# First loads on two queues, two more block pairs per FFN, input forms without 1/rms, and head 0's softmax issued earlier

## The chip, the cores and the metric

The kernel runs on one core of a Trainium2 chip. Times are device microseconds of one execution: 2015.23 us is the median of three runs before the change (2014.92 to 2015.56). In the profile PE is the engine of the matmuls, PEld its weight loads, DVE, ACT and POOL the vector, scalar and GpSimd engines, SP the engine from whose queue nearly all loads are issued.

## The reference

The program is a trunk of two layers for 512 tokens of width 1024, all in float32:

```python
def rms_norm(x, g):
    return x * lax.rsqrt(jnp.mean(x * x, axis=-1, keepdims=True) + NORM_EPS) * g

def swiglu(x, w_gate, w_up, w_down):          # 1024 -> 2816 -> 1024
    return (jax.nn.silu(x @ w_gate) * (x @ w_up)) @ w_down

for layer in range(2):
    h = h + 0.5 * swiglu(rms_norm(h, ffn_norm[layer, 0]), ...)
    u = rms_norm(h, mix_norm[layer])
    h = h + (mla_gla_mixer(u, ...) if layer % 2 == 0 else nsa_mixer(u, ...))
    h = h + 0.5 * swiglu(rms_norm(h, ffn_norm[layer, 1]), ...)
return rms_norm(h, final_norm)
```

The NSA mixer has 16 heads of 64 in 4 groups. A head's output is the gated sum of three softmax branches: over 31 compressed keys, over selected key blocks, and over a window. For 512 tokens the selection and the window hold every causal key, so the last two branches are plain causal softmaxes over their own keys.

## The kernel before

Activations lie transposed, features on the 128 partitions and the 512 tokens along the row; x is eight tiles `x0` to `x7`. To keep float32 accuracy every operand is split in a high and a low part, and `mm3` (lines 145 to 147) makes each product of three matmuls: high by high, high by low, low by high. `split` (lines 150, 151) makes the parts: ACT casts the high one, DVE subtracts it to get the low one. Each weight tile (`raw`, 512 KB, three buffers) is loaded by SP's queue and split so.

There are four FFNs, FFN0 to FFN3; the MLA and GLA mixer stands between the first two, the NSA mixer between the last two. An FFN has 22 column blocks of 128, each a gate and an up product, called a pair here. Pairs come in two kinds.

A whole pair (`whole`, j < `NP` = 6) has two products of 8 by 3 matmuls with 512 columns, from x times the gain alone (`xs`, made by `ffn_input`); 1/rms (`rb`) is not needed for these, and comes in when DVE evicts them (line 386, `gt` and `ut`). The first eviction thus waits for `rb`, and since the tag `gu` has four PSUM banks, two for a pair, the third whole pair waits for the first eviction.

A block pair (`gate_up` and `gate_up_steps`, the other 16) is a two-by-two block product in Winograd's form: seven products of 12 matmuls with 256 columns in place of eight. It needs sums of weights (`sa`, `sb`, lines 130 to 133, and their splits `shi`, `slo`) and seven forms of the input (`ffn_forms`). The forms are made from x times gain times `rb`, 16 operations on DVE at line 282, three subtractions, and seven splits. At a pair's end ACT applies Silu to each half of `gt` (lines 334, 349), DVE multiplies (`done`, line 363), and `hid[j]` is split for the down product.

Down products (`unit`, `ps_d`) of a group of four or five finished pairs are put between the pairs of the next group, and the last group's run behind the last pair. FFN3 ends in `ffn_end`, which works on halves of the tokens with the last four `hid`.

The order of instructions on each engine is fixed when the program is built, by a list scheduler that goes by a model of ready times and priorities. `tc.high_priority(AHEAD)` moves a few evictions ahead, `issue_after` holds an instruction back in this order. `bufs=n` says how many buffers a tag shares: a load into `raw` waits until the tile three loads earlier has been read.

In the NSA mixer `nsa_keys_queries` makes the projections row by row; after row `CMP_AFTER` it issues `cmp_probs`, the compressed branch's probabilities of the first group. `nsa_attend` then runs the heads; `probs(h)` holds a head's 14 score matmuls, its softmax blocks, and POOL's weighing by the gates (line 584).

At the start SP issues all loads: x0, the gains, the first weight in four parts, x1 to x7, then masks and tables, and only then the second weight.

Of the kernel before, what the change touches and what calls it, by code (L numbers as in the profile page):

```python
# [29 lines left out]
NP = 6  # L30
# [9 lines left out]
class Core:  # L40


    def __init__(self, ctx, tc, a):
        self.ctx, self.tc, self.nc, self.a = ctx, tc, tc.nc, a
        nc = self.nc
        ep = lambda name, bufs, **k: ctx.enter_context(tc.tile_pool(name=name, bufs=bufs, **k))
        self.cp = ep("const", 1)
        self.xp = ep("resid", 1)
        self.sp = ep("scr", 1)
        self.wp = ep("wts", 1, side="right")  # L50
        cp = self.cp
# [4 lines left out]
        self.inv_dm = self.const_col(1.0 / DM, "inv_dm")  # L56
        table = cp.tile([P, 1], F32, name="table")
        nc.scalar.activation(table, self.ones[:, :1], AF.Identity, scale=self.inv_dm)
        self.gains = cp.tile([P, 7, KC], F32, name="gains")
        self.x = []  # L60
        for k in range(KC):
            self.x.append(self.xp.tile([P, T], F32, name=f"x{k}"))
        self.open_sums()
# [5 lines left out]
    def load_x(self, k0, k1):  # L69
        for k in range(k0, k1):  # L70
            self.nc.sync.dma_start(out=self.x[k], in_=self.a["xT"][:, k])
# [164 lines left out]
    def ffn(self, f, gi, meanwhile=None, out=None, act_last=False):  # L236

        if f:
            self.open_sums()
        with self.fws, ExitStack() as st:  # L240
            if act_last:
                hp = st.enter_context(self.pool("hid"))
            self.open_act(st, 14)
            self.open_psum(st, gu=4, d=3, st=1)
            if not act_last:
                hp = st.enter_context(self.pool("hid"))
            fp = st.enter_context(self.pool("fin")) if out is not None else None
            self.ffn_body(f, gi, hp, meanwhile, fp, out)
# [22 lines left out]
    def ffn_forms(self, gi, hp, parts):  # L271

        V = self.nc.vector
        b11, b12, b21, b22, t = (hp.tile([P, 4, H], F32, name="xf", tag="hid", bufs=HID) for _ in range(5))
        for kh, bs in enumerate(((b11, b12), (b21, b22))):
            for th, b in enumerate(bs):
                for kk in range(4):
                    k = 4 * kh + kk  # L280
                    ts = slice(th * H, th * H + H)
                    V.scalar_tensor_tensor(
                        out=b[:, kk], in0=self.x[k][:, ts], scalar=self.gains[:, gi, k : k + 1], in1=self.rb[:, ts], op0=ALU.mult, op1=ALU.mult,
                    )
            yield

        def add(b):
            parts.append((self.form("bh"), self.form("bl")))
            self.split(b, *parts[-1])

        V.tensor_sub(t, b22, b12)
        add(b11)
        yield
        add(b21)
        add(t)
        yield
        V.scalar_tensor_tensor(out=t, in0=t, scalar=-1.0, in1=b11, op0=ALU.mult, op1=ALU.subtract)
        V.scalar_tensor_tensor(out=b21, in0=t, scalar=-1.0, in1=b21, op0=ALU.mult, op1=ALU.subtract)
        V.tensor_sub(b12, b11, b12)
        yield  # L300
        for b in (t, b21, b12, b22):
            add(b)

    def product(self, ps, w, x, start=False):

        for kk in range(4):
            m = slice(kk * P, (kk + 1) * P)
            self.mm3(ps, w[0][:, m], w[1][:, m], x[0][:, kk], x[1][:, kk], start and kk == 0, kk == 3, skip_group_check=True)

    def gate_up_steps(self, hp, w, x, done):  # L310
# [37 lines left out]
        with tc.high_priority(AHEAD):  # L348
            S.activation(gt[:, H:], z, AF.Silu)
        done(gt, ut)  # L350

    def ffn_body(self, f, gi, hp, meanwhile, fp, out):
# [5 lines left out]
        acc = self.sumsq(self.x, fast=True) if self.first else None  # L358
# [3 lines left out]
        def done(j, gt, ut):  # L362
            V.tensor_mul(ut, gt, ut)
# [3 lines left out]
        def whole(j):  # L367
# [14 lines left out]
            if self.rb is None:  # L382
                self.rb = self.norm_stats(acc)[1]
# [19 lines left out]
        making = self.ffn_forms(gi, hp, forms)  # L403
# [638 lines left out]
class Mix1(Mix0):  # L1042
    def ffn_mix1(self):

        a = self.a
        with ExitStack() as left, ExitStack() as right:
            with self.pool("rope1", side="right") as tp:
# [3 lines left out]
                with ExitStack() as pj:  # L1051
# [3 lines left out]
                    with self.pool("cmp") as cq:  # L1055
                        rb = self.nsa_cmp(mp, cq, xh, xl)
                        self.nsa_gates(mp, cq, xh, xl, rb)
                    self.open_act(left, 16, "kq")
                    ks, qs = self.nsa_keys_queries(mp, xh, xl)
            at = right.enter_context(self.pool("nsa_at", side="right"))  # L1060
            self.open_psum(right, s=3, pt=3, av=1, pj=1)
            oh, ol = self.nsa_attend(mp, at, ks, qs)
# [164 lines left out]
    def nsa_keys_queries(self, mp, xh, xl):  # L1227
# [31 lines left out]
        for row, scale, store, args in steps:  # L1259
# [7 lines left out]
        return ks, qs  # L1267
# [41 lines left out]
    def nsa_attend(self, mp, at, ks, qs):  # L1309
# [4 lines left out]

        def probs(h):

            g = h // 4
            sums = at.tile([P, 2, 4], F32, name="sums", tag="sums", bufs=2)
            kh, kl = ks[g]
            out = [at.tile([P, 1280], F32, name="pr", tag="pr", bufs=4) for _ in range(2)]  # L1320

            def block(br, qb, ps):
                n = (qb + 1) * P
                self.softmax_block(ps, n, out[br][:, OFF[qb] : OFF[qb] + n], sums[:, br, qb : qb + 1], mp, "f")

# [172 lines left out]
```

## Time and profile before

| | |
|---|---|
| median of 3 runs | 2015.23 us |
| the profiled execution's own time | 2016.61 us |
| its span, first to last instruction | 2014.6 us |
| PE busy | 1969.8 us (98%) |
| DVE busy | 1496.0 us (74%) |
| ACT busy | 1020.9 us (51%) |
| POOL busy | 212.8 us (11%) |
| mean granted TensorE clock | 0.990 |

The profile shows one execution; a row of the timeline gives the start from the span's beginning, the length, the engine, the source line, what was written from what, and in brackets how long the engine had stood idle and what released it. Matmuls overlap, so the time of one is read from start to start, not from its length.

### The profile page before, as it was taken

The page shows a single profiled execution, that of the slowest core. Times are in us where ns is not written, and L with a number is a line of the kernel's source. Part 1 is how long each engine was busy: PE and PEld are TensorE (multiplying, and loading weights), DVE is VectorE, ACT ScalarE, POOL GpSimd, SP SyncE. Part 2 cuts the span into 40 slices and gives each one's busy share as a digit, 9 for nine tenths or more (in the row PEclk, how much of TensorE's full clock was granted, in tenths as well). Part 3 has the DMA queues.
Part 4 walks back from the last instruction along what each step waited for, and adds up shares of the span by engine and source line. Part 5 has one row for each costly group of instructions (what it writes and reads, how often), then busy time and mean ns, then how long its engine had stood idle before and what let it go on. Part 6 is the DMA issues. An engine that isn't in the chain of part 4 may idle for free.

```text
span 2014.6 us, 31364 instructions
## 1 busy us (share of the span) xinstructions
PE 1969.8 (98%) x11934; PEld 1737.3 (86%) x11934; DVE 1496.0 (74%) x2571; ACT 1020.9 (51%) x1850; POOL 212.8 (11%) x258
## 2 busy tenths in 40 slices
PE   8999999999999999999999999999899999999997
PEld 6899999898778899998789999888687878999997
DVE  7877775688888677775877777677899868777764
ACT  6444443665674444444544444445588754444443
POOL 0000000201340000001000000111266510000002
PEclk9999999999999999999999999999899999999999
DMA  5233322321313232323323233354400133233332
GB/s 173 89 98 102 101 96 79 109 74 44 88 66 113 89 101 90 117 91 89 121 89 96 94 106 103 90 146 135 116 2 1 33 112 97 86 102 96 102 96 67
DMA packets 71910, 186.40 MB, mean 93 GB/s; under 512 B 9936, under 2 KB 13648, under 8 KB 71760
## 3 DMA queue, kind: packets, MB, share of 16 engines
q1 hardware_dynamic: 71760, 184.41, 29.5%
q8 instruction: 93, 1.52, 0.3%
q14 instruction: 57, 0.47, 0.1%
HBM read 172.84 MB, written 2.10 MB: 87 GB/s over the span
## 4 chain that ended last, share of the span: by engine, by line
PE 89%; DVE 5%; ACT 2%; issue 1%; DMA 1%; SPq 1%; POOL 0%; DVEq 0%; ACTq 0%; POOLq 0%
PE ps_d L145 8%; PE ps_d L146 8%; PE ps_d L147 8%; PE ps_a L145 6%; PE ps_a L147 6%; PE ps_a L146 6%; PE ps_b L145 5%; PE ps_b L147 5%; PE ps_b L146 5%; PE ps_gu L146 5%; PE ps_gu L145 5%; PE ps_gu L147 4%; PE ps_p L145 3%; PE ps_p L146 2%; PE ps_p L147 2%; PE ps_pt L593 2%
## 5 line engine op out<-in xcount | busy, mean ns | idle before, releaser
L150 ACT CAST whi<-raw 128x512 fp32r<-128x512 f32 (+4 forms) x319 | 257.7, 811 | 333.5 <-PE ps_d L146 126.6
L151 DVE TENSOR_TENSOR wlo<-raw,whi 128x512 fp32r<-128x512 f32 (+4 forms) x319 | 308.2, 968 | 84.6 <-ACT whi L150 83.6
L145 PE MATMUL ps_d<-hid,whi 128*128 128x512 f32 x672 | 265.1, 398 | 0.0
L146 PE MATMUL ps_d<-hid,whi 128*128 128x512 f32 x672 | 264.2, 394 | 0.0
L147 PE MATMUL ps_d<-hid,wlo 128*128 128x512 f32 x672 | 263.9, 394 | 0.0
L145 PE MATMUL ps_a<-bh,shi 128*128 128x256 f32 x768 | 217.0, 282 | 0.0
L146 PE MATMUL ps_a<-bl,shi 128*128 128x256 f32 x768 | 216.4, 282 | 0.0
L147 PE MATMUL ps_a<-bh,slo 128*128 128x256 f32 x768 | 216.2, 281 | 0.0
L215 POOL TENSOR_TENSOR ssq<-ssq,sq 128x512 f32<-128x512 f32 x30 | 46.3, 1545 | 1093.9 <-ACT sq L214 1093.9
L147 PEld LDWEIGHTS ps_d<-hid,wlo 128*128 128x128 f32 x672 | 126.1, 188 | 30.4 <-DVE wlo L151 0.7
L145 PEld LDWEIGHTS ps_d<-hid,whi 128*128 128x128 f32 x672 | 126.1, 188 | 26.4 <-ACT whi L150 1.0
L146 PEld LDWEIGHTS ps_d<-hid,whi 128*128 128x128 f32 x672 | 126.1, 188 | 24.4
L146 PEld LDWEIGHTS ps_a<-bl,shi 128*128 128x128 f32 x768 | 144.8, 189 | 1.2
L145 PEld LDWEIGHTS ps_a<-bh,shi 128*128 128x128 f32 x768 | 144.1, 188 | 1.3
L147 PEld LDWEIGHTS ps_a<-bh,slo 128*128 128x128 f32 x768 | 145.0, 189 | 0.0
L130 DVE TENSOR_TENSOR sa<-raw 128x512 f32<-128x512 f32 x64 | 44.2, 690 | 130.7 <-DMA raw<-wgu 130.6
L398 DVE SCALAR_TENSOR_TENSOR x<-ps_d,x 128x512 f32<-128x512 f32 x152 | 104.2, 687 | 44.1 <-PE ps_d L147 43.8
L584 POOL TENSOR_TENSOR pr<-pr,sums 128x128 f32<-128x128 f32 (+3 forms) x160 | 114.4, 747 | 106.7 <-DVE sums L1342 42.6
L150 ACT CAST uhi<-raw 128x512 fp32r<-128x512 f32 x64 | 39.7, 621 | 163.5 <-PE ps_b L146 102.9
L150 ACT CAST shi<-sa 128x1024 fp32r<-128x1024 f32 x64 | 67.2, 1050 | 81.5 <-PE ps_a L146 73.0
L151 DVE TENSOR_TENSOR slo<-sa,shi 128x1024 fp32r<-128x1024 f32 x64 | 78.3, 1224 | 33.5 <-ACT shi L150 33.4
L565 ACT ACTIVATE pr<-sm_s,sm_m 128x512 f32<-128x512 f32 (+3 forms) x160 | 90.2, 565 | 17.4 <-DVE sm_m L561 13.4
(448 smaller groups left out, 5583.6 us busy)
## 6 DMA issues: line engine op xcount, KB each, us to landing
raw<-wgu SPq DMA_DIRECT2D x175, 512.0 KB, 3.8
raw<-wd SPq DMA_DIRECT2D x96, 256.0 KB, 2.7
raw<-wd SPq DMA_DIRECT2D x64, 320.0 KB, 3.0
raw<-wo SPq DMA_DIRECT2D x32, 256.0 KB, 2.8
raw<-w1t SPq DMA_DIRECT2D x16, 512.0 KB, 3.7
raw<-w0v SPq DMA_DIRECT2D x8, 512.0 KB, 3.6
raw<-w0t SPq DMA_DIRECT2D x6, 512.0 KB, 3.9
rt_s<-rt_f SPq DMA_DIRECT2D x48, 64.0 KB, 2.0
```

The costliest lines, as they stand in the source:

```text
L130: V.tensor_add(av[:, :w], g[:, :w], u[:, :w])
L145: mm(ps, lh, rh, start=start, stop=False, **k)
L146: mm(ps, lh, rl, start=False, stop=False, **k)
L147: mm(ps, ll, rh, start=False, stop=stop, **k)
L150: self.nc.scalar.copy(hi, src)
L151: self.nc.vector.tensor_sub(lo, src, f32v(hi))
L215: (nc.vector if last or fast else nc.gpsimd).tensor_add(acc, acc, sq)
L398: V.scalar_tensor_tensor(out=self.x[c], in0=ps, scalar=0.5, in1=self.x[c], op0=ALU.mult, op1=ALU.add)
L565: nc.scalar.activation(p, s[:, :n], AF.Exp, bias=mn, scale=-1.0, accum_out=sums)
L584: self.nc.gpsimd.tensor_mul(o, o, w[:, qb : qb + 1].to_broadcast([P, n]))
L593: self.nc.tensor.transpose(ps[:, off : off + P], prs[br][:, o : o + P], self.ident)
```

## The change

The first loads use two queues: ACT issues x0, x1 and x2 with x3, SP the gains, the first weight in two parts, x4 with x5 and x6 with x7. Eleven small matmuls of ones by ones are issued ahead of FFN0's first product. `NP` is 4, so each FFN has 4 whole and 18 block pairs. The forms of the input are made without `rb`: three of the seven are views of `xs`, four are made from x times gain by one operation or more, and `rb` is multiplied in at the end of a block pair: DVE multiplies `gt` by it, POOL multiplies `ut`, ACT applies Silu over the full width, and POOL makes the product of both. `nsa_probs` of head 0 is issued inside `nsa_keys_queries`, with the PSUM tag `ch`; the later `cmp_probs` are held back behind the preceding head's score matmuls. The kernel is built with a DMA scratch size of 1024.

```diff
-NP = 6
+NP = 4
+WARM = 11
...
+        load(nc.scalar, 0, 1)
+        nc.sync.dma_start(out=self.gains, in_=a["gains"])
+        load(nc.scalar, 1, 2)
+        self.first = self.wload(a["wgu"][0, 0, 0], 1024, parts=2)
+        load(nc.scalar, 2, 4)
+        load(nc.sync, 4, 6)
+        load(nc.sync, 6, 8)
...
-        self.load_x(0, 1)
-        nc.sync.dma_start(out=self.gains, in_=a["gains"])
-        self.first = self.wload(a["wgu"][0, 0, 0], 1024, parts=4)
-        self.load_x(1, KC)
...
-            self.open_act(st, 14)
+            self.open_act(st, 17 if out is not None else 16)
...
+        for kk in range(4):
+            S.activation(b12[:, kk], block(kk, 1), AF.Copy, scale=gain(kk))
+        parts.append(view(0, 0))
+        parts.append(view(1, 0))
+        combine(t3, 1, 1, b12, ALU.subtract)
+        form(t3, False)
         yield
+        combine(t2, 0, 0, t3, ALU.add)
+        form(t2, True)
         yield
+        combine(t2, 1, 0, t2, ALU.subtract)
+        form(t2, True)
         yield
+        combine(b12, 0, 0, b12, ALU.subtract)
+        form(b12, False)
+        parts.append(view(1, 1))
...
             V.tensor_add(gt[:, :H], vv, sa)
-            S.activation(gt[:, :H], gt[:, :H], AF.Silu)
...
         with tc.high_priority(AHEAD):
-            S.activation(gt[:, H:], z, AF.Silu)
+            S.copy(gt[:, H:], z)
+        V.tensor_mul(gt, gt, self.rb)
+        nc.gpsimd.tensor_mul(ut, ut, self.rb)
+        S.activation(gt, gt, AF.Silu)
         done(gt, ut)
...
         def done(j, gt, ut):
-            V.tensor_mul(ut, gt, ut)
+            (V if j < NP else nc.gpsimd).tensor_mul(ut, gt, ut)
...
+        if f == 0:
+            ps = self.ps("warm", "st")
+            for _ in range(WARM):
+                nc.tensor.matmul(ps[:, :P], self.ones, self.ones, start=True, stop=True)
...
             if row == CMP_AFTER:
                 self.pc0 = self.cmp_probs(mp, qs, 0, "ch")
+                first = self.nsa_probs(mp, self.ap, ks, qs, 0, "ch")
...
-                    pc[(h + 1) // 4] = self.cmp_probs(mp, qs, (h + 1) // 4, "pj")
-                nxt = probs(h + 1)
+                    with self.tc.issue_after(end.ins):
+                        pc[(h + 1) // 4] = self.cmp_probs(mp, qs, (h + 1) // 4, "pj")
+                nxt = self.nsa_probs(mp, at if (h + 1) % 3 else self.ap, ks, qs, h + 1, "s")
```

Three places show how the instructions move. The first is DVE in FFN1, around the first eviction (`gt` from `ps_gu`; line 386 before, 397 after). Before:

```order
L202 TENSOR_SCALAR rs_q<-rs_q 128x4
L203 TENSOR_TENSOR rc<-rc,rs_q 128x4
L182 TENSOR_SCALAR dg<-ident,rc 128x128 x4
L151 TENSOR_TENSOR wlo<-raw,whi 128x1024
L386 TENSOR_TENSOR gt<-ps_gu,rb 128x512
L386 TENSOR_TENSOR ut<-ps_gu,rb 128x512
```

After:

```order
L203 TENSOR_TENSOR rc<-rc,rs_q 128x4
L182 TENSOR_SCALAR dg<-ident,rc 128x128 x4
L151 TENSOR_TENSOR wlo<-raw,whi 128x1024
L130 TENSOR_TENSOR sa<-raw 128x512
L131 TENSOR_TENSOR sa<-raw 128x512
L397 TENSOR_TENSOR gt<-ps_gu,rb 128x512
L397 TENSOR_TENSOR ut<-ps_gu,rb 128x512
```

The `wlo` is that of the fourth pair's gate weight in both; the two sums of pair 5's weights now stand between it and the eviction. FFN2 has the same rows.

The second is ACT at the end of FFN3's last pair (`gt` from `ps_a`, then the cast of its `hid`; `keep` are the last down weights, `facc` the final norm's first square). Before:

```order
L150 CAST keep<-raw 128x512
L334 ACTIVATE gt<-gt 128x256
L339 COPY sx<-ps_a 128x256
L150 CAST keep<-raw 128x512 x3
L349 ACTIVATE gt<-ps_a 128x256
L150 CAST hid<-ut 128x512
```

After:

```order
L150 CAST keep<-raw 128x512 x2
L358 COPY gt<-ps_a 128x256
L361 ACTIVATE gt<-gt 128x512
L150 CAST hid<-ut 128x512
L473 ACTIVATE facc<-x 128x256
```

Between the last read of `ps_a` and the cast of `hid` there is now a full-width Silu on ACT, with DVE's product by `rb` ahead of it and POOL's product behind it.

The third is PE where the NSA projections end: `ps_s` are a head's scores, `ps_sc` and `ps_sct` belong to a group's compressed probabilities, `ps_pc` to their transposes, `ps_av` to the values. Before:

```order
L1304 MATMUL ps_pc<-ident,sc_s 128x128 x4
L1328 MATMUL ps_s<-kh,q 128x256
L1329 MATMUL ps_s<-kl,q 128x256
L1337 MATMUL ps_s<-kh,q 128x256
...
L1353 MATMUL ps_av<-pcl,vcz 128x512
L1279 MATMUL ps_sc<-q,kcwh 128x512
...
L1284 MATMUL ps_sct<-ident,sc_t 128x128 x4
L1337 MATMUL ps_s<-kh,q 128x512
```

After:

```order
L1321 MATMUL ps_pc<-ident,sc_s 128x128 x4
L1339 MATMUL ps_s<-kh,q 128x256
L1340 MATMUL ps_s<-kl,q 128x256
L1348 MATMUL ps_s<-kh,q 128x256
...
L1349 MATMUL ps_s<-kl,q 128x384
L1369 MATMUL ps_av<-pch,vcz 128x512
L1370 MATMUL ps_av<-pcl,vcz 128x512
L608 MATMUL ps_pt<-ident,pr 128x128 x2
```

The second group's `ps_sc` and `ps_sct` no longer stand among head 0's scores; the scores themselves still begin behind `ps_pc`.

## Rows read from the trace of the kernel before

**Rows 1.** Page, parts 1 and 4: busy time by engine, chain by engine.

```profile
PE 1969.8 (98%) x11934; PEld 1737.3 (86%) x11934; DVE 1496.0 (74%) x2571; ACT 1020.9 (51%) x1850; POOL 212.8 (11%) x258
...
PE 89%; DVE 5%; ACT 2%; issue 1%; DMA 1%; SPq 1%; POOL 0%; DVEq 0%; ACTq 0%; POOLq 0%
```

**Rows 2.** Stretches: core's length, then busy us of each engine, clock, DMA share, GB/s.

```profile
200.00:345.00 145.00, 145.00 (x984) 134.11 (x983) 99.00 (x145) 61.11 (x104) 0.00 (x0) 1.00 0.31 95
```

**Rows 3.** Timeline of PE: start, length, matmul, [idle before]; a whole and a block pair.

```profile
624.05 0.40 PE L145 MATMUL ps_gu<-xh,whi 128*128 128x512 f32 x1
...
629.65 0.40 PE L145 MATMUL ps_gu<-xh,shi 128*128 128x512 f32 x1
...
252.54 0.28 PE L145 MATMUL ps_a<-bh,shi 128*128 128x256 f32 x1
...
253.98 0.28 PE L145 MATMUL ps_a<-bh,whi 128*128 128x256 f32 x1
```

**Rows 4.** Timeline of PE and of SP's queue in FFN0's first 40 us.

```profile
9.17 0.79 PE L145 MATMUL ps_gu<-xh,whi 128*128 128x512 f32 x1 [2.12 <-ACT xh L265]
...
15.15 0.43 PE L145 MATMUL ps_gu<-xh,whi 128*128 128x512 f32 x1
...
10.00 0.33 SPq L91 DMA_DIRECT2D raw<-wgu  x1
...
38.12 0.50 PE L145 MATMUL ps_gu<-xh,whi 128*128 128x512 f32 x1 [1.64 <-DVE gt L386]
```

**Rows 5.** Stretches, as rows 2: hand-over from projections to attention, and attention.

```profile
1440.00:1470.00 30.00, 22.45 (x83) 15.99 (x82) 25.41 (x68) 18.30 (x47) 11.96 (x14) 0.66 0.26 64
...
1500.00:1575.00 75.00, 70.50 (x438) 59.07 (x437) 72.02 (x229) 66.43 (x184) 45.40 (x64) 1.00 0.01 1
```

**Rows 6.** Lines: sx's copy (200 to 345 us); POOL's sums, ns min/median/max.

```profile
L339 ACT COPY sx<-ps_a 128x256 f32<-128x256 f32 x9 | 3.3, 370 | 0.9 <-PE ps_a L147 0.8
...
L215 POOL TENSOR_TENSOR ssq<-ssq,sq x30: 1288/1476/2350, 356.0 to 1642.1; 128x512 f32<-128x512 f32 x30
```

**Rows 7.** Line 226's durations; timeline of POOL and DVE near 365 us.

```profile
L226 DVE SCALAR_TENSOR_TENSOR xl<-x,gains,xh x16: 739/742/1786, 356.4 to 1312.8; 128x512 fp32r<-128x512 f32 x16
...
364.71 2.35 POOL L215 TENSOR_TENSOR ssq<-ssq,sq 128x512 f32<-128x512 f32 x1 [1.76 <-ACT sq L214]
...
364.69 1.21 DVE L151 TENSOR_TENSOR wlo<-raw,whi 128x1024 fp32r<-128x1024 f32 x1
...
365.82 1.78 DVE L226 SCALAR_TENSOR_TENSOR xl<-x,gains,xh 128x512 fp32r<-128x512 f32 x1
```

**Rows 8.** Timeline of PE, DVE and ACT at the end of FFN3's pairs.

```profile
1977.43 0.28 PE L147 MATMUL ps_a<-bh,slo 128*128 128x256 f32 x1
...
1978.16 0.69 DVE L363 TENSOR_TENSOR ut<-gt,ut 128x512 f32<-128x512 f32 x1 [2.83 <-ACT gt L349]
...
1978.89 0.62 ACT L150 CAST hid<-ut 128x512 fp32r<-128x512 f32 x1 [0.76 <-DVE ut L363]
...
1979.56 0.62 PE L145 MATMUL ps_d<-hid,keep 128*128 128x256 f32 x3 [0.30 <-ACT hid L150]
```

**Rows 9.** Timeline of PE at the end of FFN0's pairs.

```profile
348.24 0.28 PE L147 MATMUL ps_a<-bh,slo 128*128 128x256 f32 x1
...
351.39 0.86 PE L145 MATMUL ps_d<-hid,whi 128*128 128x512 f32 x3
```

**Rows 10.** Timeline of DVE in FFN1; page, part 6: loads of gate and up weights.

```profile
618.70 1.23 DVE L151 TENSOR_TENSOR wlo<-raw,whi 128x1024 fp32r<-128x1024 f32 x1 [1.60 <-ACT whi L150]
...
622.31 0.69 DVE L386 TENSOR_TENSOR gt<-ps_gu,rb 128x512 f32<-128x512 f32 x1 [2.39 <-ACT rb L167]
...
raw<-wgu SPq DMA_DIRECT2D x175, 512.0 KB, 3.8
```

**Rows 11.** Stretches, as rows 2, behind two waits of PE.

```profile
38.00:48.00 10.00, 9.88 (x42) 8.00 (x43) 10.00 (x23) 5.62 (x8) 0.00 (x0) 1.00 0.16 52
...
376.90:380.40 3.50, 3.50 (x19) 3.50 (x19) 2.48 (x11) 0.95 (x2) 0.00 (x0) 0.52 0.46 147
```

More of the change, by code (lines that the diff above doesn't have):

```diff
@@ L269, in ffn_input, with ffn_forms, view, combine @@
         return xs, end
[L271 to L292, printed above, removed]
+    def ffn_forms(self, gi, hp, xs, parts):
+        V, S = self.nc.vector, self.nc.scalar
+        b12, t3, t2 = (hp.tile([P, 4, H], F32, name="xf", tag="hid", bufs=HID) for _ in range(3))
+        gain = lambda k: self.gains[:, gi, k : k + 1]
+        block = lambda k, th: self.x[k][:, th * H : th * H + H]
+        def view(kh, th):
+            return [tuple(t[:, th * H : th * H + H] for t in xs[4 * kh + kk]) for kk in range(4)]
+        def combine(out, kh, th, t, op):
+            for kk in range(4):
+                k = 4 * kh + kk
+                V.scalar_tensor_tensor(out=out[:, kk], in0=block(k, th), scalar=gain(k), in1=t[:, kk], op0=ALU.mult, op1=op)
+        def form(t, negated):
+            h, l = self.form("th"), self.form("tl")
+            if negated:
+                S.activation(h, t, AF.Copy, scale=-1.0)
+                V.scalar_tensor_tensor(out=l, in0=t, scalar=-1.0, in1=f32v(h), op0=ALU.mult, op1=ALU.subtract)
+            else:
+                self.split(t, h, l)
+            parts.append([(h[:, kk], l[:, kk]) for kk in range(4)])
+        for kk in range(4):
+            S.activation(b12[:, kk], block(kk, 1), AF.Copy, scale=gain(kk))
[3 more added lines that the diff above has]
+        form(t3, False)
@@ L1307, in cmp_probs, with nsa_probs, block, nsa_attend @@
         return ph, pl
-    def nsa_attend(self, mp, at, ks, qs):
+    def nsa_probs(self, mp, pool, ks, qs, h, tag):
+        V, mm = self.nc.vector, self.nc.tensor.matmul
+        sums = mp.tile([P, 2, 4], F32, name="sums", tag="sums", bufs=3)
+        kh, kl = ks[h // 4]
+        out = [pool.tile([P, 1280], F32, name="pr", tag="pr", bufs=2 if pool is self.ap else 4) for _ in range(2)]
+        def block(br, qb, ps):
+            n = (qb + 1) * P
+            self.softmax_block(ps, n, out[br][:, OFF[qb] : OFF[qb] + n], sums[:, br, qb : qb + 1], self.ap, "sm")
+        ps = self.ps("ps_s", tag)
+        o = ps[:, : 2 * P].rearrange("p (b n) -> p b n", b=2)
+        mm(o, qs[h][:, :P], kh[:, :, :P], start=True, stop=False)
+        mm(o, qs[h][:, :P], kl[:, :, :P], start=False, stop=True)
+        for br in range(2):
+            block(br, 0, ps[:, br * P : (br + 1) * P])
+        for br in range(2):
+            for qb in range(1, 4):
+                n = (qb + 1) * P
+                ps = self.ps("ps_s", tag)
+                qt = qs[h][:, qb * P : n]
+                mm(ps[:, :n], qt, kh[:, br, :n], start=True, stop=False)
+                end = mm(ps[:, :n], qt, kl[:, br, :n], start=False, stop=True)
+                block(br, qb, ps)
+            w = sums[:, br]
+            V.scalar_tensor_tensor(out=w, in0=w, scalar=TINY, in1=self.inv_gates[:, h, br], op0=ALU.max, op1=ALU.mult)
+            V.reciprocal(w, w)
+            self.weigh(out[br], w)
+        return out, end
+    def nsa_attend(self, mp, at, ks, qs, nxt):
         nc, a = self.nc, self.a
```

66 lines of the change are left out of this document (14 added, 52 removed).

## The prediction

> **What bounds the kernel now.** I read the busy shares first, then the chain that ended last, then every idle gap of PE in the timeline, then the stretches around the edits. PE is busy 1969.8 of 2014.6 us and is 89% of the chain [rows 1]; DVE has 74%, ACT 51%, POOL 11%. So only two things can save time: fewer PE cycles, or shorter waits of PE, which stands still 44.8 us in all, with the stretches at its lower clock around them. Work on DVE, ACT or POOL counts only where PE waits for it. Inside the steady part of the FFNs PE never waits: in 200 to 345 us it is busy 145.00 of 145.00 while DVE has 99.00 and ACT 61.11 [rows 2]. The gaps lie at the start, at the first evictions of FFN0, in the small stages of the mixers and above all where the NSA projections hand over to attention.
>
> **The change part by part.** Times are against the profiled execution, span 2014.6 us; the median of the runs, 2015.23, is 0.63 above that span, and I add that at the end.
>
> *Two more block pairs in each FFN.* A whole pair is 48 matmuls of 512 columns; 24 of them take 629.65 − 624.05 = 5.60 us, so a pair takes 11.20. A block pair is 7 products of 12 matmuls of 256 columns; 12 take 253.98 − 252.54 = 1.44, so a pair takes 10.08 [rows 3]. Saved: 1.12 a pair, times 2 pairs, times 4 FFNs: **−8.96**. This is PE time proper, and the order of the products within a pair is unchanged. DVE pays more for a block pair's weights: three splits of 1024 and five operations of 512, 3 × 1.23 + 5 × 0.69 = 7.1 [rows 8, 10], where a whole pair has two splits, 2.5; twice an FFN, 9.2. The new forms give most of that back: seven splits and three full-size sums become four splits, six times 1.23 = 7.4 less, and they no longer wait for 1/rms. PE never waited for them, so this is 0 while DVE has its 31% idle; without that cover the rest, 1.8 an FFN, would be the price.
>
> *The start.* Before, PE has three matmuls from 5.34, waits 2.12 for x1 and runs on from 9.17; the second weight is asked for at 10.00, behind x, cmask and the rope table on SP; matmuls stand 0.43 apart up to 15.15 and 0.23 after, the two clock levels [rows 4]. Now x comes on two queues in larger pieces, u0 is asked for around 5, and 11 small matmuls run ahead. The first 24 products, of which nine are left at 15.15 before and end near 17.3, end near 16.0 by my walk, and the wait for slo behind them goes. The end of whole(1), its rb chain and the first eviction, for which PE waits 1.64 at 38.12 [rows 4], follow as a block; behind them two sums for pair 5 now stand ahead of that eviction, worth about 0.25. I take **−1.3**. Bounds: 0 if both queues share the same bandwidth and x1 comes as late as before; −3.5 if PE runs from 5.6 on or is at the upper clock from 9 on (13 matmuls by 0.2 = 2.6, and the rest from the waits).
>
> *NSA.* The diff speaks of head 0 among the projections; the order says otherwise: its 14 score matmuls still stand behind the last projection and the four ps_pc transposes. What leaves the hand-over is the second group's compressed probabilities: 8 score matmuls, 8 transposes, about 2.7 us of PE and 5 us of DVE, which go into attention. The 30 us from 1440 to 1470 have DVE busy 25.41, so 4.6 idle, and PE busy 22.45 at a mean clock of 0.66; attention behind it has DVE 72.02 of 75 and PE 70.50 [rows 5]. Work moved from a stretch where DVE is nearly full to one where both are nearly full can win at most the idle time, 4.6, plus some clock; it loses where the moved part splits a head's softmax: +2. Head 0's first sums come about 5.5 to 6.5 earlier by DVE's queue, 5 are paid back. I take **−2**.
>
> *The end of a block pair.* Now ACT copies (sx's copy: 0.370), DVE multiplies gt by rb, ACT does Silu over the full width, and POOL does ut·rb and gt·ut. POOL's 128x512 sums took 1.288 to 2.350, median 1.476 [rows 6]. In 72 pairs that is 2 × 1.48 × 72 = 213 us on an idle engine. Two costs follow.
>
> First, the two engines hold each other up. An xl, made from x and xh in SBUF, has a median of 742 ns but 1786 at most, and that one, from 365.82, lies beside a POOL sum of 2.35 from 364.71, itself 1.06 over the shortest. The wlo begun at 364.69 has its usual 1.21 [rows 6, 7]. Read in order: POOL stood behind wlo, then xl behind POOL. So each of POOL's two operations can cost DVE from 0 to 1.29, and I take 0.75 of that, the share of DVE's operations with both inputs in SBUF (an estimate from its list): 1.9 per pair. Nine pairs end in the 145 us [rows 2, 6], 16.1 each, so DVE goes from 68% to about 80%: **0**, covered by PE.
>
> Second, hid of the last pair comes later. In FFN3 the last ps_a matmul begins at 1977.43, gt·ut on DVE at 1978.16 (0.69), and ps_d's first use of that hid at 1979.56, after a wait of 0.30 [rows 8]. Now the chain is copy 0.37, gt·rb 0.69, Silu 0.62 (as hid's cast of that width [rows 8]), POOL 1.29, hid 0.62 with their hand-overs: about 1981.5. **+2.0**, all on the path since what lies ahead of it in PE's order is used up. In FFN0 the last ps_a begins at 348.24 and the first use of its hid stands at 351.39, so 3.15 of other products cover it [rows 9]; the chain needs 0.37 + 0.69 + 0.62 + 1.29 + 0.62 and four hand-overs of 0.1: 4.0. **+0.9** in each of three FFNs, **+2.7**. Bounds: 0.5 to 2.0 each, the upper one where POOL's product stands behind a DVE split as in rows 7, 1.06 more.
>
> [...]
>
> *The first evictions of FFN1 and FFN2.* Pair 5's two sums (lines 130, 131) now stand ahead of the first gt eviction on DVE, and they need the twelfth raw tile, u5. Its buffer comes free only when wlo of g3 has been made: 618.70 + 1.23 = 619.93 in the trace of before. A 512 KB load takes 3.8 from issue to landing [rows 10], so u5 lands at 623.7, the sums end at 625.0, the eviction at 625.7. Before, the eviction is at 622.31 [rows 10] and whole(2) starts at 624.05 with no wait [rows 3]. Queued behind: that eviction and through it PE. **+1.6** in FFN1 and, by the same order, FFN2: **+3.2**. Bounds 0 (load in 2.2) and +5 (load crowded). In FFN3 the first eviction stands ahead of those sums, so nothing.
>
> *The DMA scratch size* changes no instruction: 0.
>
> Sum: −8.96 − 1.3 − 2.0 + 2.0 + 2.7 + 3.2 = −4.36, a span of 2010.2 and a median of **2010.9**.
>
> **Rivals.** *A, the new waits are covered:* u5 lands in time and the three FFN tails keep 0. Then −8.96 − 1.3 − 2.0 + 2.0 = −10.3, and with the start's better end −12.5: 2003 to 2005. For it: 3.8 is a median over loads in busier stretches too, and PE had no wait at either place. Against: both chains are sums of serial steps, each from a row.
>
> *B, the clock falls behind the new waits (slower).* [...] Behind the wait of 1.64 at 38.12 [rows 4] it stays at 1.00 [rows 11]; PE had wide matmuls before that one. The change adds six waits of 0.9 to 2 us (four tails, two evictions). [...] By its surroundings a tail or eviction is like 38.12, so I give this little. [...]
>
> *C, NSA gives nothing or loses* (the change does not do there what it says): the second group's probabilities cost attention 5 us of DVE, the hand-over gains 5: C between 0 and +2 in place of −2: 2013 to 2015, not to be told from no change.
>
> **How the numbers follow.** A measurement tells 0.2%, 4 us. Chances: forecast 0.46 (own range 2007.5 to 2014, by the bounds of start, tails and evictions), A 0.18, B 0.15, C 0.21. Faster by over 0.2% means under 2011.2: A whole and 0.7 of the forecast, whose median lies there, 0.18 + 0.32 = 0.50. Slower means over 2019.3: the upper half of B, 0.08, and 0.04 of C for a DVE-bound attention: 0.12. Same: 0.38. The range leaves out half of A's faster end and B's upper part: 2003.5 to 2018.
>
> **What would show it.** In the trace of the changed kernel: a pair in FFN2 from 11.20 to 10.08; PE waits for hid of about 2.3 in FFN3 and about 0.9 in the others; waits of about 1.6 for gt in FFN1 and FFN2 with the L130 sums after a raw load just ahead on DVE; DVE's two-SBUF operations longer beside POOL but PE full in the pairs; the ps_s waits at the hand-over smaller and those inside attention larger; first full-rate matmul before 15. I am wrong if PE waits inside the pairs (DVE bound), if the tails show no wait, or if the granted clock has new dips.

## The result

The changed kernel takes 2029.45 us (median of five runs, 2025.9 to 2030.76), the kernel before 2015.56 in the same session: a ratio of 1.0063, 95% interval 1.0051 to 1.0074. It is slower by 13.9 us where 4.4 faster was forecast. The profiled execution is one of the quicker ones, 2026.95 with a span of 2025.2, so the traces have 10.6 us to explain. The rest lies in the spread of the runs. The medians here are of undisturbed runs; one run of the experiment with the old start, 3461.16 us at a granted clock of 0.768, is left out.

Parts 1 and 4 of the page of the changed kernel, the engines' busy time and the chain that ended last (of before in [rows 1]):

```profile
PE 1966.1 (97%) x12244; PEld 1747.2 (86%) x12244; DVE 1557.1 (77%) x2597; ACT 1047.2 (52%) x1900; POOL 425.1 (21%) x402
...
PE 84%; DVE 8%; DMA 3%; ACT 2%; issue 1%; POOL 0%; SPq 0%; ACTq 0%; DVEq 0%; POOLq 0%
```

PE has lost only 3.7 us of busy time, since the eleven small matmuls, from 1.05 to 6.11, added 5.1; its idle time has grown from 44.8 to 59.1. DVE's share of the chain went from 5 to 8%. The largest waits of PE in the changed kernel, in total, times and the longest:

```profile
PE ps_gu L145 <- DVE gt L397: 10.0, 3, 4.3
...
PE ps_s L1348 <- DVE sm_m L576: 5.3, 6, 2.8
...
PE ps_d L145 <- ACT hid L150: 5.0, 4, 2.4
...
PE ps_pc L1321 <- DVE sc_s L1318: 3.1, 1, 3.1
```

The two traces by stage, from the start times of PE's matmuls in either:

| stage | before | after | difference |
|---|---|---|---|
| start to the last down product of FFN0 | 367.64 | 371.01 | +3.37 |
| MLA and GLA mixer, to FFN1's first product | 232.19 | 229.88 | −2.31 |
| FFN1 | 353.66 | 354.39 | +0.73 |
| FFN2 | 354.15 | 359.80 | +5.65 |
| NSA mixer, to FFN3's first product | 336.56 | 336.79 | +0.23 |
| FFN3 and the final norm, to PE's last matmul | 362.95 | 365.69 | +2.74 |
| the end | 7.46 | 7.61 | +0.15 |

By the prediction's price the block pairs make each FFN 2.24 shorter, so the four lost 5.6, 3.0, 7.9 and 5.0 elsewhere.

**Where FFN2 lost it.** Timeline of DVE, SP's queue and PE at the first eviction of FFN2:

```profile
978.49 1.22 DVE L151 TENSOR_TENSOR wlo<-raw,whi 128x1024 fp32r<-128x1024 f32 x1
...
979.74 0.33 SPq L91 DMA_DIRECT2D raw<-wgu  x1
...
983.09 0.69 DVE L130 TENSOR_TENSOR sa<-raw 128x512 f32<-128x512 f32 x1 [3.38 <-DMA raw<-wgu]
...
983.70 0.69 DVE L131 TENSOR_TENSOR sa<-raw 128x512 f32<-128x512 f32 x1
...
984.30 0.68 DVE L397 TENSOR_TENSOR gt<-ps_gu,rb 128x512 f32<-128x512 f32 x1
...
985.04 0.50 PE L145 MATMUL ps_gu<-xh,whi 128*128 128x512 f32 x1 [4.28 <-DVE gt L397]
```

`wlo` ends at 979.71; SP issues the load of u5 at 979.74 into the buffer that this freed; DVE, in its fixed order, stands idle 3.38 until it has landed, makes the two sums, and only then the eviction for which PE has waited 4.28. That is the wait that the prediction described, but longer. DVE and PE in FFN2 of the kernel before, the same `wlo` and the third whole pair:

```profile
974.42 1.22 DVE L151 TENSOR_TENSOR wlo<-raw,whi 128x1024 fp32r<-128x1024 f32 x1
...
978.22 0.39 PE L145 MATMUL ps_gu<-xh,whi 128*128 128x512 f32 x1
```

From FFN2's first product, `wlo` came 20.7 us later before and comes 23.0 us later now. In both it stands behind the chain of small operations that makes 1/rms from the statistics; in the changed kernel this chain in turn stands behind pair 4's first sums, and begins at 974.04 although PE has finished the statistics at 968.74.

In FFN1 the wait fits the forecast almost to the digit (1.53 against 1.6):

```profile
620.09 1.22 DVE L151 TENSOR_TENSOR wlo<-raw,whi 128x1024 fp32r<-128x1024 f32 x1
...
624.86 0.69 DVE L130 TENSOR_TENSOR sa<-raw 128x512 f32<-128x512 f32 x1 [3.56 <-DMA raw<-wgu]
...
626.81 0.50 PE L145 MATMUL ps_gu<-xh,whi 128*128 128x512 f32 x1 [1.53 <-DVE gt L397]
```

In FFN0 the load of u5 is issued at 31.61 and the eviction has pair 4's split in front of it besides, so PE waits 4.19 where it had waited 1.64 [rows 4]:

```profile
31.61 0.33 SPq L91 DMA_DIRECT2D raw<-wgu  x1
...
36.24 0.69 DVE L130 TENSOR_TENSOR sa<-raw 128x512 f32<-128x512 f32 x1 [2.35 <-DMA raw<-wgu]
...
37.45 1.22 DVE L151 TENSOR_TENSOR slo<-sb,shi 128x1024 fp32r<-128x1024 f32 x1
...
38.59 0.68 DVE L397 TENSOR_TENSOR gt<-ps_gu,rb 128x512 f32<-128x512 f32 x1
...
39.32 0.80 PE L145 MATMUL ps_gu<-xh,whi 128*128 128x512 f32 x1 [4.19 <-DVE gt L397]
```

**The tails.** The end of FFN0's last pair on ACT, DVE, ACT, POOL, ACT and PE, and PE's row of FFN3 (of before in [rows 8, 9]):

```profile
350.74 0.37 ACT L358 COPY gt<-ps_a 128x256 f32<-128x256 f32 x1 [4.32 <-PE ps_a L147]
...
351.14 0.69 DVE L359 TENSOR_TENSOR gt<-gt,rb 128x512 f32<-128x512 f32 x1 [3.82 <-ACT gt L358]
...
351.87 0.63 ACT L361 ACTIVATE gt<-gt 128x512 f32<-128x512 f32 x1 [0.76 <-DVE gt L359]
...
352.64 1.29 POOL L374 TENSOR_TENSOR ut<-gt,ut 128x512 f32<-128x512 f32 x1 [6.69 <-ACT gt L361]
...
353.96 0.62 ACT L150 CAST hid<-ut 128x512 fp32r<-128x512 f32 x1 [1.46 <-POOL ut L374]
...
354.63 0.73 PE L145 MATMUL ps_d<-hid,whi 128*128 128x512 f32 x2 [0.90 <-ACT hid L150]
...
1987.86 0.62 PE L145 MATMUL ps_d<-hid,keep 128*128 128x256 f32 x3 [2.35 <-ACT hid L150]
```

Copy, product by `rb`, Silu, POOL's product, cast: 3.9 us in a row, and PE waits 0.90. FFN1 and FFN2 have 0.90 each as well, FFN3 2.35 where it had 0.30.

**The clock.** Stretches behind the three longest of these waits, and behind the wait for the MLA mixer's statistics; the column after the engines' busy times is the granted clock (of before in [rows 11]):

```profile
39.40:44.00 4.60, 4.60 (x11) 3.63 (x12) 4.60 (x9) 2.87 (x6) 0.00 (x0) 0.52 0.00 0
...
985.00:989.50 4.50, 4.46 (x13) 3.50 (x14) 4.50 (x7) 2.21 (x5) 0.00 (x0) 0.62 0.00 0
...
1987.90:1992.90 5.00, 4.85 (x24) 4.44 (x25) 2.05 (x5) 1.83 (x5) 1.47 (x2) 0.66 0.00 0
...
379.10:382.60 3.50, 3.50 (x31) 3.50 (x32) 2.84 (x11) 1.82 (x3) 0.00 (x0) 1.00 0.40 129
```

Behind the 4.19, the 4.28 and the 2.35 the clock is at its lower level, 0.50, for most of these stretches; from 39.40 to 43.80, at 0.50, the matmuls of 512 columns stand 0.43 apart, and from 44.04 on 0.23. The first two lose 2.2 and 1.7 us by it; in the third the same matmuls take 1.4 us longer than in the trace of before. Behind the waits of 0.90 and 1.53 it stays up (1.00 from 355 to 359 and from 627 to 631). The fourth row is the other way: before, the clock had fallen to 0.52 there. Over the whole execution the records of the clock show its lower level for 39.1 us, and for 40.1 us before: about as much went at the MLA mixer's statistics and in the NSA mixer as came here, and the mean is 0.990 in both.

The same wait came with the fall and without it. One program, run twice (it is the one with a single small matmul, below), waits 1.40 us at FFN0's first eviction both times; the stretch behind it, first run and second:

```profile
36.10:40.70 4.60, 4.60 (x20) 3.73 (x21) 4.60 (x9) 2.82 (x6) 0.00 (x0) 1.00 0.00 0
...
36.10:40.70 4.60, 4.60 (x13) 3.66 (x14) 4.60 (x8) 2.81 (x6) 0.00 (x0) 0.63 0.00 0
```

### The profile page after: what moved, and what is told of

It reads as the page before. It is cut to its first block, busy times and chain, and to the rows that moved or that the text cites. A ratio compares the mean times of both kernels' runs of the same rounds, so it can differ in the third digit from the quotient of the medians.

```text
span 2025.2 us, 32193 instructions
## 1 busy us (share of the span) xinstructions
PE 1966.1 (97%) x12244; PEld 1747.2 (86%) x12244; DVE 1557.1 (77%) x2597; ACT 1047.2 (52%) x1900; POOL 425.1 (21%) x402
## 3 DMA queue, kind: packets, MB, share of 16 engines
q10 hardware_dynamic: 432, 1.05, 0.2%
## 4 chain that ended last, share of the span: by engine, by line
PE 84%; DVE 8%; DMA 3%; ACT 2%; issue 1%; POOL 0%; SPq 0%; ACTq 0%; DVEq 0%; POOLq 0%
PE ps_d L145 7%; PE ps_d L146 7%; PE ps_d L147 7%; PE ps_a L145 7%; PE ps_a L147 7%; PE ps_a L146 7%; PE ps_b L145 5%; PE ps_b L146 5%; PE ps_b L147 5%; PE ps_p L145 3%; PE ps_p L146 3%; PE ps_p L147 3%; PE ps_gu L145 2%; PE ps_gu L146 2%; PE ps_gu L147 2%; DMA raw<-wgu 2%
## 5 line engine op out<-in xcount | busy, mean ns | idle before, releaser
L150 ACT CAST whi<-raw 128x512 fp32r<-128x512 f32 (+3 forms) x317 | 257.5, 816 | 396.9 <-DMA raw<-wd 201.5
L151 DVE TENSOR_TENSOR wlo<-raw,whi 128x512 fp32r<-128x512 f32 (+3 forms) x317 | 313.0, 990 | 97.4 <-ACT whi L150 96.0
L360 POOL TENSOR_TENSOR ut<-ut,rb 128x512 f32<-128x512 f32 x72 | 112.4, 1560 | 593.1 <-DVE ut L355 531.2
L145 PE MATMUL ps_a<-th,shi 128*128 128x256 f32 x576 | 163.0, 283 | 0.1
L146 PE MATMUL ps_a<-tl,shi 128*128 128x256 f32 x576 | 162.4, 282 | 0.0
L147 PE MATMUL ps_a<-th,slo 128*128 128x256 f32 x576 | 161.9, 281 | 0.0
L151 DVE TENSOR_TENSOR slo<-sb,shi 128x1024 fp32r<-128x1024 f32 x72 | 115.0, 1597 | 4.3 <-ACT shi L150 4.3
L145 PEld LDWEIGHTS ps_a<-th,shi 128*128 128x128 f32 x576 | 108.0, 187 | 2.0 <-ACT sx L348 0.9
L146 PEld LDWEIGHTS ps_a<-tl,shi 128*128 128x128 f32 x576 | 108.5, 188 | 1.0
L147 PEld LDWEIGHTS ps_a<-th,slo 128*128 128x128 f32 x576 | 109.0, 189 | 0.0
```

The costliest lines, as they stand in the source:

```text
L145: mm(ps, lh, rh, start=start, stop=False, **k)
L146: mm(ps, lh, rl, start=False, stop=False, **k)
L147: mm(ps, ll, rh, start=False, stop=stop, **k)
L150: self.nc.scalar.copy(hi, src)
L151: self.nc.vector.tensor_sub(lo, src, f32v(hi))
L360: nc.gpsimd.tensor_mul(ut, ut, self.rb)
```

## The experiments

**Evictions first.** Pair 5's first two sums are held behind the first pair's evictions:

```diff
-                V.tensor_mul(t, pt[s], self.rb)
+                ev = V.tensor_mul(t, pt[s], self.rb)
+                if j == 0:
+                    self.first_evict = ev
...
+            if j == NP + 1:
+                st.enter_context(self.tc.issue_after(self.first_evict.ins))
             V.tensor_add(av[:, :w], g[:, :w], u[:, :w])
             V.tensor_add(av[:, w:], u[:, :w], u[:, w:])
```

> The changed kernel, with pair 5's first two weight sums (sa) issued only after the first whole pair's evictions in every FFN; nothing else differs. In the changed kernel the third whole pair starts after waits of 4.19, 1.53 and 4.28 us in FFN0, FFN1 and FFN2. Theory (the eviction is queued on DVE behind sums that wait for a load that itself waits for a free raw buffer): the waits fall to about 1.4, 0 and 0.3, and the stretches at half clock behind the two long ones (2.2 and 1.7 us lost) go too: 8 to 12 us faster than the changed kernel, so 2 to 6 us slower than before. Rival (the evictions were late for another reason, rb or the PSUM banks): the waits stay, no change against the changed kernel, 14 us slower than before.

Measured: 2017.35 us, 12.1 below the changed kernel and 1.0008 (0.9998 to 1.0018) of before; span 2015.2, 10.0 less. DVE's first eviction in FFN0 with the first sum now behind it, the stretch after it, and PE's waits for `gt` in total:

```profile
35.36 0.69 DVE L400 TENSOR_TENSOR gt<-ps_gu,rb 128x512 f32<-128x512 f32 x1
...
37.77 0.68 DVE L133 TENSOR_TENSOR sa<-raw 128x512 f32<-128x512 f32 x1
...
36.20:40.80 4.60, 4.60 (x20) 3.74 (x21) 4.60 (x9) 2.81 (x6) 0.00 (x0) 1.00 0.00 0
```

```profile
PE ps_gu L148 <- DVE gt L400: 2.3, 3, 1.4
```

The eviction comes at 35.36 instead of 38.59, the waits fall from 10.0 to 2.3, and the granted clock behind it is 1.00 where it was 0.52. The theory holds, with its upper number: the order of two sums on DVE cost more than the block pairs save.

**Short tail.** In each FFN's last pair alone, POOL does nothing and half of the work is done early:

```diff
+            if last:
+                V.tensor_mul(gt[:, :H], gt[:, :H], self.rb[:, :H])
+                S.activation(gt[:, :H], gt[:, :H], AF.Silu)
...
+        if last:
+            with tc.high_priority(AHEAD):
+                V.tensor_mul(ut, ut, self.rb)
+                V.tensor_mul(gt[:, H:], z, self.rb[:, H:])
+                S.activation(gt[:, H:], gt[:, H:], AF.Silu)
...
-            (V if j < NP else nc.gpsimd).tensor_mul(ut, gt, ut)
+            (V if j < NP or j == JC - 1 else nc.gpsimd).tensor_mul(ut, gt, ut)
```

> The changed kernel, with the end of each FFN's last pair alone done otherwise: the first half of gt gets rb and its Silu early, DVE makes ut*rb early and, after the last product, z*rb for the second half straight from PSUM and gt*ut; POOL does nothing in this pair. Theory (POOL's product and the full-width Silu stand in the chain to the last hid): the waits of 0.90 in FFN0, FFN1 and FFN2 go to 0 and the 2.35 in FFN3 to 0.8, with the stretch at half clock behind it: 4 to 5.5 us faster than the changed kernel. If the wait ahead of the MLA mixer's statistics, 0.46 in the changed kernel and 1.06 before, comes back with its stretch at half clock, only 2 to 3. Rival (the tails are bound by ACT's queue, not by POOL): waits unchanged, no difference.

Measured: 2022.54 us, 6.9 below the changed kernel, 1.0030 (1.0021 to 1.0040) of before; the spans differ by 3.7. PE's waits for `hid` in the first three FFNs are gone, and in FFN3 there is left, timeline of PE:

```profile
1985.95 0.62 PE L145 MATMUL ps_d<-hid,keep 128*128 128x256 f32 x3 [0.79 <-ACT hid L150]
```

0.79 where 0.8 was expected, and the clock stays up behind it. The theory holds as to the waits. Of the time, 4 to 5.5 us were expected; the medians give more and the spans less, since the changed kernel's profiled run was a quick one.

**NSA as before.** The diff is that of the change's NSA part, backwards.

> The changed kernel with the NSA part of the kernel before: head 0's softmax issued after the projections, the second group's compressed probabilities not held back, four pr buffers in one pool. Theory (what left the hand-over came back in attention: PE time lost over its matmuls' usual spacing is 13.7 instead of 16.6 at the hand-over, 14.3 instead of 10.0 in attention): 0 to 1.5 us faster than the changed kernel. Rival (the prediction's -2 for this part): 2 us slower than the changed kernel.

Measured: 2027.66 us, 1.8 below the changed kernel, with intervals that overlap (1.0033 to 1.0063 and 1.0051 to 1.0074), so the medians alone don't decide. In the traces the time from the start of the last projection's last matmul to that of FFN3's second matmul is 205.11 with the old form and 206.57 with the new: 1.5 less. The other traces bear this out. Five have the new form, with 205.53 to 206.98 us, 206.4 in the mean; eight have the old one, the kernel before among them, with 204.33 to 205.71, 204.8 in the mean. PE's waits there, old form (to be read beside those of the changed kernel above):

```profile
PE ps_pc L1319 <- DVE sc_s L1316: 3.5, 2, 2.8
...
PE ps_s L1352 <- DVE sm_m L576: 3.2, 5, 2.2
```

The new form waits 5.3 for `sm_m` instead of 3.2. The forecast gain of 2 isn't there; the part costs about 1.6 us.

**Six whole pairs.** `NP = 6` in the changed kernel.

> The changed kernel with six whole pairs per FFN instead of four; new forms, start, ends and NSA stay. Theory (it is the preparation of pair 5, drawn into the time of the first evictions by NP = 4, that makes them late): the first evictions are on time again, the waits of 4.19, 1.53 and 4.28 fall by 8 in all and their half-clock stretches by 3.8, and the eight block pairs give back 9.0: about 3 us faster than the changed kernel. Rival (the evictions are late whatever NP is): 9 us slower than the changed kernel.

Measured: 2026.03 us, 3.4 below the changed kernel. PE's waits:

```profile
PE ps_gu L145 <- DVE gt L397: 1.9, 1, 1.9
...
PE ps_d L145 <- ACT hid L150: 5.0, 4, 2.3
```

One wait for `gt` is left, FFN0's, with 1.9; the tails stay as they were, though the clock this time stays up behind FFN3's 2.35. With `NP` at 6 the sums of the first block pairs come later than the evictions. So it was the smaller number of whole pairs that drew pair 5's sums to this place, and the sum fits: 9.0 more for the pairs, 12.1 less for the evictions.

**No POOL in the pairs.** Both of POOL's products are DVE's in all block pairs.

```diff
-        nc.gpsimd.tensor_mul(ut, ut, self.rb)
+        V.tensor_mul(ut, ut, self.rb)
...
-            (V if j < NP else nc.gpsimd).tensor_mul(ut, gt, ut)
+            V.tensor_mul(ut, gt, ut)
```

> The changed kernel with POOL's two products at the end of every block pair made by DVE instead. Theory (in the steady pairs PE covers whatever DVE does, so POOL's cost is only its length in the chain of the last pair): DVE gains 2 x 0.69 of work a pair and loses the stretching by POOL, about nothing; the waits for hid fall from 0.90 to 0.2 in three FFNs and from 2.35 to 1.7 in FFN3, 2.8 us faster than the changed kernel in all. Rival 1 (POOL and DVE holding each other up costs PE time all along): 5 us or more faster. Rival 2 (DVE becomes the bound in the pairs): slower than the changed kernel, with PE waits inside the pairs.

Measured: 2027.66 us, 1.8 below. Stretch of FFN0's pairs, PE, PEld, DVE, ACT, POOL, in the changed kernel and then without POOL:

```profile
200.00:340.00 140.00, 139.79 (x951) 128.64 (x950) 103.07 (x142) 62.66 (x104) 23.85 (x18) 1.00 0.31 97
```

```profile
200.00:340.00 140.00, 140.00 (x954) 129.59 (x953) 107.89 (x160) 63.52 (x104) 0.00 (x0) 1.00 0.32 97
```

PE's waits without POOL:

```profile
PE ps_gu L145 <- DVE gt L397: 9.6, 3, 4.3
...
PE ps_d L145 <- ACT hid L150: 4.7, 4, 2.0
```

PE is full in the pairs in both, so neither rival holds. But the tails hardly gain: the chain is 0.6 shorter, but PE's order has less cover ahead of it (in FFN0 nine matmuls of other products where there were thirteen), so the waits are 1.13, 1.13, 0.43 and 2.03. POOL's two products cost the kernel next to nothing.

**The three together.** Evictions first, short tail, NSA as before.

> The changed kernel with the three edits of the earlier runs at once: pair 5's sums behind the first evictions, the short chain at the end of each FFN's last pair, the NSA part of the kernel before. Theory (three separate losses of the change): they add, 12.1 + 6.9 + 1.8 = 20.8 us faster than the changed kernel's 2029.45, so about 2009, 0.3% faster than before. Rival (what one edit saves comes back as another wait, at the mixers' statistics or in the clock): 2012 to 2015, no difference from before that can be told.

Measured: 2011.08 us, 0.9973 (0.9963 to 0.9983) of before: 4.3 faster than before and 18.4 faster than the changed kernel, where the three edits alone gave 20.8. They nearly add.

**One small matmul for eleven**, on the kernel of the three fixes.

```diff
-WARM = 11
+WARM = 1
```

> The kernel of the three fixes with one small matmul ahead of FFN0 instead of eleven. Theory (the eleven bring the upper clock forward, matmuls 0.23 apart from about 10 instead of 15 us): without them the first products stand 0.43 apart until about 14, and the u products begin 1.0 to 1.7 us later; 1 to 1.7 us slower than with eleven. Rival (the start is bound by when x and the weights land, not by the clock): no change.

Measured: 2006.72 us, 0.9955 (0.9939 to 0.9971): faster, where slower had been expected. Timeline of PE at the start, first with eleven, then with one:

```profile
9.65 0.50 PE L148 MATMUL ps_gu<-xh,whi 128*128 128x512 f32 x1 [1.26 <-ACT xh L268]
...
10.78 0.39 PE L150 MATMUL ps_gu<-xh,wlo 128*128 128x512 f32 x1
...
11.01 0.40 PE L148 MATMUL ps_gu<-xh,whi 128*128 128x512 f32 x1
...
13.81 0.63 PE L149 MATMUL ps_gu<-xl,whi 128*128 128x512 f32 x1
...
14.24 0.63 PE L150 MATMUL ps_gu<-xh,wlo 128*128 128x512 f32 x1
...
16.20 0.40 PE L148 MATMUL ps_gu<-xh,shi 128*128 128x512 f32 x1
```

```profile
10.34 0.40 PE L150 MATMUL ps_gu<-xh,wlo 128*128 128x512 f32 x1
...
10.57 0.40 PE L148 MATMUL ps_gu<-xh,whi 128*128 128x512 f32 x1
...
14.60 0.39 PE L148 MATMUL ps_gu<-xh,shi 128*128 128x512 f32 x1
```

With eleven, the matmuls stand 0.23 apart at 10.78, but 0.43 at 13.81, and the second weight's products begin at 16.20. With one they stand 0.23 apart from 10.34 on, and those products begin at 14.60. In the changed kernel's trace 0.23 was the spacing at 1.00 and 0.43 that at 0.50. The 22 rows of the eleven take 4.44 us here, 0.21 apart at first and 0.11 from 4.8 on, where they took 5.06 in the changed kernel's trace, 0.21 apart to the end: the upper clock came earlier with them than with one. But PE then waits 1.26 for x, and behind it, from 12.96 to 14.66, the matmuls stand 0.43 apart again. Of the eight traces with eleven, three lost the upper clock in this way, behind waits for x of 1.01, 1.12 and 1.26, and their second weight's products began at 16.00 to 16.20; five kept it, with waits of 0.64 to 1.02, and began at 14.68 to 14.99. So the eleven gain nothing. Whether they cost 4 us was still open, so both kernels ran again side by side.

> The kernel of the three fixes with one small matmul ahead instead of eleven, again, beside the one with eleven. Theory (the eleven gain nothing: the second weight's products began at 14.60 without them and at 16.20, 14.90 and 14.68 with them; the rest of the 4.4 us between the two medians lies in half-clock stretches elsewhere that come and go): within 2 us of the kernel with eleven. Rival (the eleven cost time at the start): 3 to 5 us faster than with eleven.

> The kernel of the three fixes with eleven small matmuls, again, beside the one with one. Theory: 2009 to 2011, within 2 us of the kernel with one. Rival: 3 to 5 us slower than that.

Measured: 2012.42 us with one, 0.9966 (0.9952 to 0.9979), and 2009.41 with eleven, 0.9961 (0.9948 to 0.9973). The order is reversed, so no difference can be told; the same program gave 2006.72 and 2012.42 in two sessions, beside 2015.35 and 2016.87 for the kernel before, which is the limit of such comparisons here. The trace of the second has four stretches at the lower clock, 3.4 to 6.8 us long, ahead of the hand-over to attention, that of the first one.

**The old start**, on the three fixes: first loads of the kernel before, no small matmuls.

> The kernel of the three fixes with the first loads of the kernel before: all from SP's queue, x in eight pieces, the first weight in four, no small matmuls ahead. Theory (the new start ends the second whole pair 1.9 us earlier, 33.45 against 35.36): 1.5 to 2.5 us slower than the three fixes. Rival (the third pair waits for rb or for a load at that place in any case): 0 to 0.5 us slower, the difference coming back as a shorter wait for the first eviction.

Measured: 2010.37 us, 0.9977 (0.9965 to 0.9989), against 2011.08 and, in the second session, 2009.41: the medians can't tell them apart. The third pair starts at 37.29, and at 36.81 and 36.24 in the two traces with the new start. So the new loads bring 0.5 to 1.1 us there, less than the theory's 1.5, and at or above the rival's 0.5.

**Six whole pairs, all mended.** `NP = 6` on the kernel with the three fixes and one small matmul.

> The kernel of the three fixes with one small matmul ahead, and six whole pairs per FFN instead of four. Theory (a block pair in place of a whole one saves 1.12 us of PE, and with the evictions mended nothing else hangs on the number): eight whole pairs more cost 9.0 us, so about 2015.5, no difference from before. Rival (the block pairs' extra DVE work costs back part of it in the first evictions or in the forms): 3 to 6 us slower than with four, 2010 to 2013.

Measured: 2020.24 us, 1.0019 (1.0010 to 1.0028) of before. Against the two medians with four whole pairs, 2006.72 and 2012.42, that is 7.8 to 13.5 more; 9.0 lies inside. By stage, the traces differ by 1.7 to 2.8 in each of FFN1 to FFN3, where 2.24 was expected, but by 5.4 and 7.0 in FFN0, where the one with six pairs also waits 1.36 for a copy of ACT in the midst of the pairs. So the price of a pair holds in three FFNs; why FFN0 pays more was not tried. Nothing suggests that block pairs give part of their gain back.

## Why the prediction was wrong

The forecast was 2010.9 and the median 2029.45, 18.6 more. By the experiments the evictions make 8.7 of this, the NSA part 3.6, the tails with the clock behind them 2.2 and the start up to 0.8; 3 to 4 us are left.

*Block pairs, −8.96: right.* The mended kernel with six whole pairs is slower by 7.8 or more, and by 1.7 to 2.8 in three of its FFNs.

*The first evictions: the step that failed.* The mechanism stood in the prediction, with its place and its chain, and FFN1 was right (1.53 for 1.6). But its price was read from FFN1 alone and carried to FFN2 "by the same order", without walking FFN2's own rows: there `wlo` ends at 975.64 and the third pair starts at 978.22, and the same sum gives 981.4, a wait of 3.2 instead of 1.6. The rest, to 4.28, is a second omission: the walk took `wlo` from the trace of before, and pair 4's sums, which the change puts ahead of the statistics' chain, make it 2.3 later. In FFN1 that chain begins 2.0 later too, counted from the FFN's first product, but there DVE had stood idle for 1.60 ahead of `wlo` [rows 10], which took up most of it; so the 1.53 is right in its mechanism and in part lucky in its size. In FFN0, where I had put 0.25 for the two sums, the load of u5 landed late too and the wait rose by 2.55. So the term was +8.4 instead of +3.45, and the clock's fall behind the two long waits made it 12.1 by the experiment.

*The tails: right.* 0.90 three times for 0.9, and 2.35 in FFN3, 2.05 above before, for +2.0. The upper bound, 2.0 each, with POOL's product standing behind a split of DVE as in [rows 7], was not reached: POOL's product took 1.29 in FFN0 and 1.26 in FFN3, and no operation of DVE ran beside it.

*The clock, rival B: underweighted.* It was given 0.15, with the reason that a wait between wide matmuls, such as the 1.64 at 38.12, leaves the clock up. That is so for 0.90 and 1.53. It isn't for FFN3's 2.35, a size that the prediction itself had named, nor for 4.19 and 4.28, which it had not. The three stretches lose 5.3 us together, 1.4 to 2.2 each. And 1.64 at that place was one draw: in nine traces with a wait of 1.40 to 1.91 there, the clock fell in four. The new dips were one of the signs of being wrong that the prediction gave; that other dips went in exchange, it did not foresee.

*NSA, −2: wrong in sign*, +1.6 by the traces, as rival C had it. What left the hand-over came back in attention, whose waits for `sm_m` grew.

*The start, −1.3: about right for what it counted.* Whole(1) ended 1.9 earlier; the eviction behind it swallowed it. With the evictions mended, 0.5 to 1.1 were left. The eleven small matmuls, which it counted in, gave nothing.

*POOL beside DVE: right that PE covers it.* Page rows of the changed kernel, pair sums and a split with POOL running beside them:

```profile
L151 DVE TENSOR_TENSOR slo<-sb,shi 128x1024 fp32r<-128x1024 f32 x72 | 115.0, 1597 | 4.3 <-ACT shi L150 4.3
...
L130 DVE TENSOR_TENSOR sa<-raw 128x512 f32<-128x512 f32 x72 | 66.4, 922 | 49.7 <-DMA raw<-wgu 49.4
```

Without POOL the same groups have means of 1218 for the split and 691 for the sum. The prediction counted only operations with both inputs in SBUF as held up. The changed kernel's trace fits this: `slo` from `sb` and `shi` took 1207 to 2319 ns, while `gt` from `ps_b` and `sa`, with one input in PSUM, took 408 to 426 in all 72 pairs. DVE works 103.07 of 140 us in the stretch shown above, 74%, where 80% was forecast.

*Not foreseen:* the MLA mixer is 2.3 shorter. PE's wait for the statistics is 0.46, where it was 1.06:

```profile
378.96 1.05 PE L178 MATMUL ps_s<-inv_dm,ssq 128*128 128x1 f32 x8 [0.46 <-DVE ssq L215]
```

and the clock stays up behind it, as the stretch from 379.10 shows. Why the statistics came earlier was not tried; in the twelve traces of changed kernels this stage takes from 229.88 to 233.20, so what the one trace gains is within what comes and goes. The new forms of the input and the scratch size were not tried by themselves.

By stage, with the traces' numbers: FFN0 has −2.24 for the pairs, −1.9 for the start, +2.55 for the eviction, +2.2 for the clock behind it, +0.90 for the tail and +0.58 for a new wait ahead of the product that spreads 1/rms, 2.1 of the 3.37 measured. FFN1 has −2.24, +1.53 and +0.90, 0.2 of 0.73. FFN2 has −2.24, +4.28, +1.7 and +0.90, 4.6 of 5.65. NSA and FFN3 have −2.24, +2.05, +1.4 behind the tail, +1.8 from the last projection to FFN3's second matmul, −0.7 before it and +0.7 in the final norm, together the 2.97 measured. With the −2.31 of the MLA mixer these make 7.6 of the 10.6, and 3.0 us in the first three FFNs stay unassigned. So do the 3.3 us between the two comparisons, 13.9 of the medians and 10.6 of the traces.

## What to carry to other kernels

When a change makes a planner prepare work earlier, look what that work stands in front of on an engine whose order is fixed, and walk the chain at every place where it recurs with that place's own rows: the same order gave 1.5, 2.6 and 4.3 us. A short instruction that waits for a load should not stand ahead of one that frees a PSUM bank. Two long waits of PE were paid twice here, once as idle time and once in the clock behind them: the 4.19 and 4.28 us cost 2.2 and 1.7 more.

## What the runs showed of the hardware

In the changed kernel the granted clock fell to 0.50 at waits of 4.19, 4.28 and 2.35 us amid matmuls of 512 and 256 columns, and cost 2.2, 1.7 and 1.4 us behind them; it did not fall at 1.53 or 0.90. Over all thirteen traces it fell at each of eight waits of 3.85 to 4.33 us at the first evictions, at four of five waits of 2.03 to 2.35 at FFN3's tail, and at four of nine of 1.40 to 1.91 at FFN0's first eviction; the same program with the same wait of 1.40 had a mean clock of 0.63 in the 4.60 us behind it in one run and 1.00 in another, a difference of 1.7 us between two runs.

With eleven small matmuls ahead of the first products the matmuls had the upper clock's spacing from 4.8 us on in one trace, with one small matmul from 10.34; but in three of the eight traces with eleven it was lost again behind waits for x of 1.01 to 1.26 us; in the other five, with waits of 0.64 to 1.02, it was not.

With two POOL products in each pair, the mean of DVE's split of `sb` was 1597 ns instead of 1218, and that of the first weight sum 922 instead of 691; the split of `sa` had 1219 with them and 1223 without.
